# Stores of the transposed blocks and of the softmax heads' outputs: issued from ScalarE's queue in place of SyncE's

## The chip, the cores and the metric

One core of a Trainium2 chip runs the whole program. The metric is the device time of one execution in microseconds. The engines are called by the names of the profile: PE (TensorE), DVE (VectorE), ACT (ScalarE), POOL (GpSimd) and SP (SyncE). Each works through its own list of instructions in order; they wait for one another by semaphores. A DMA is an instruction too: it stands in the list of the engine that issues it, and it is issued when that engine comes to it and its semaphores are there. "SPq" and "ACTq" in the trace are these issues.

## The reference

One layer of a decoder on 512 tokens with 2048 columns, all float32. Cut to what matters:

```python
h = rms_norm(x, norm1_g)
proj = h @ w_in                      # columns of two groups of heads
out_a = gla_mixer(qa, ka, va, ra, log_g, onorm_g)      # 4 heads of gated linear attention
out_b = dilated_mixer(rms_norm(qb), rms_norm(kb), vb, rel_bias)  # 8 softmax heads, 3 dilations
x = x + concat(out_a, out_b) @ w_out
h2 = rms_norm(x, norm2_g)
x = x + (silu(h2 @ w_gate) * (h2 @ w_up)) @ w_down     # 5632 hidden columns
```

## The kernel before

**The products.** All large matrix products go through one scheme. A pair of 512-column blocks of a weight matrix is multiplied for all 512 tokens by seven products of half-sized blocks (`PRODUCTS`, P1 to P7; a Strassen-like scheme), whose left operands are blocks of the activations and sums of them (`A11`, `A12`, `A22`, `S1` to `S4`). Each product runs over up to four groups of 256 rows; one such step is called an item here. For an item the weights (or a difference of two weight blocks, made by DVE at L256) are split in a high part `wh`, which ACT casts (L331), and a rest `wl`, which DVE subtracts (L335). PE multiplies with 8 matmuls that read `wh` and then 4 that read `wl` (L367). `wh` and `wl` have two buffers each, so the cast for the next item can begin when PE has read the `wh` of the item before. The left operands are split in the same way in `Operand.split`: ACT casts (L174), DVE subtracts (L175).

**The stages.** First the projections with `w_in` (to 563 us of the profile), with the attention heads run between the items; then the product with `w_out` (to 734 us), then eleven pairs of `w_gate` and `w_up` (to about 1556 us, called the feed-forward stage here), then `w_down`.

**The turned rows.** A result has tokens on the partitions; the next product needs columns there. `transposed_store` (L1122 to L1145) does this for a 256-token half: for each of two column blocks, 8 transposes on PE (L1129, 4 into each half of a bank), copies from PSUM to a tile on ACT (L1137, or two with a scale at L1140), and a 256 KB store to a DRAM tensor (L1144). It writes three kinds: `mix_d` from the tile `turned` (the gated heads, called from `final_gate`), `xn_d` from `oT` and `PT` (the normalized rows after `w_out`, by `scaled_store`) and `p_d` from `oT` and `PT` (the feed-forward products). Each block is read back in the layout of an operand by `part` (L1193, tiles `r` and `top`) or `fetch_part` (L1237, tiles `v`, `T`, `qT`, `kT`, `oT`, `PT`); such a load waits until the store that it reads has landed.

**The softmax heads.** `dil_head` runs two heads side by side (lanes). ACT copies each 128-column block of the output into `ot` (L1022; the tile is called `oT` in lane 0 and `r` in lane 1), and after the last one `ot` is stored to `mix_d` (L1035). `early_jobs` loads these rows as `top` (L1193) and makes operands of them; `late_jobs` makes the sums.

**The order.** `load` and `store` are both `nc.sync.dma_start`: all loads and stores of the program but three small loads at the start stand in SP's queue, in one order. The program's order on each engine is made by a scheduler from the order of the program text and its own estimates; only the first pair of projections has an order written out by hand. So a change of the issuing engine can also move other instructions.

Of the kernel before, what the change touches and what calls it, by code (L numbers as in the profile page):

```python
# [107 lines left out]
def block_kernel(ctx: ExitStack, tc: tile.TileContext, ins, out):  # L108
    nc = tc.nc
# [18 lines left out]
    def nm(s):  # L128
        uid[0] += 1
        return f"{s}_{uid[0]}"  # L130

    def dram(shape, name):
        return dr.tile(shape, F32, name=name, tag=name)

    def bank():
        return ps.tile([P, 512], F32, name=nm("bank"), tag="bank")

    def work(tag, shape=(P, 512), bufs=1):
        return mp.tile(list(shape), F32, name=nm(tag), tag=tag, bufs=bufs)

    def const(shape, name):
        return cp.tile(list(shape), F32, name=name, tag=name)
# [2 lines left out]

    load = nc.sync.dma_start
    store = nc.sync.dma_start

    mats = const([P, 4, P], "mats")
    ident, tri, stri, causal = (mats[:, i, :] for i in range(4))  # L150
# [229 lines left out]
    def soon(fn, groups=1):  # L380

        soonest.append([groups, fn])
# [445 lines left out]
    mix_d = [dram([P, 2, 512], f"mix_d{b}") for b in range(8)]  # L828

    def head_cols(src, h, w=P):  # L830
        return src.rearrange("(t p) c -> p t c", p=P)[:, :, h * w : (h + 1) * w]
# [117 lines left out]
    def dil_head(h, lane):  # L949


        s = h // 4

        def tile_(name):
            if lane == 0:
                return work("oT" if name == "o" else name)
            if name in "qk":
                return work(name + "T")
            return rpool.tile([P, 512], F32, name=nm("r"), tag="r")

        def logits(b):
            if lane == 0:
                return work("L", bufs=2)
            return tile_("L") if b % 2 else work("PT")

        qh, kh, vh = tile_("q"), tile_("k"), tile_("v").rearrange("p (t d) -> p t d", t=4)
        load(qh.rearrange("p (t d) -> p t d", t=4), head_cols(proj[f"qb{s}"], h % 4))
        load(kh.rearrange("p (t d) -> p t d", t=4), head_cols(proj[f"kb{s}"], h % 4))
        load(vh, head_cols(proj[f"vb{s}"], h % 4))
        tb = tile_("T")  # L970
        load(tb, bass.AP(
            tensor=rep_d.tensor, offset=h * P * NB + P - 1, ap=[[NB - 1, P], [1, 512]]
        ))
        yield
        for src, g in ((qh, gq), (kh, gk)):
            tp = bank()
            for t in range(4):
                nc.tensor.transpose(tp[:, t * P : (t + 1) * P], src[:, t * P : (t + 1) * P], ident)
            nc.scalar.activation(src, tp, AF.Copy, scale=g)
        yield  # L980
        ot = tile_("o")
        lgs = {}

        def scores(b):
            n = P * (b + 1)
            lp = bank()
            nc.tensor.matmul(lp[:, :n], qh[:, b * P : (b + 1) * P], kh[:, :n], start=True, stop=True)  # L987
            lg = lgs[b] = logits(b)
            st = work("mx", (P, 4), bufs=4)

            def rest():
                nc.vector.tensor_tensor_reduce(
                    lg[:, :n], lp[:, :n], tb[:, 512 - n :], -1.0, 3.0e38, ALU.add, ALU.min,
                    st[:, 0:1],
                )
                nc.scalar.activation(
                    lg[:, :n], lg[:, :n], AF.Exp, scale=-1.0, bias=st[:, 0:1],
                    accum_out=st[:, 2:3],
                )

                def scaled():
                    nc.vector.reciprocal(st[:, 3:4], st[:, 2:3])
                    nc.vector.tensor_scalar(lg[:, :n], lg[:, :n], st[:, 3:4], None, op0=ALU.mult)

                soon(scaled)

            return rest

        def turn(b, tp):
            n = P * (b + 1)  # L1010
            for k in range(b + 1):
                nc.tensor.transpose(
                    tp[:, k * P : (k + 1) * P], lgs[b][:, k * P : (k + 1) * P], ident
                )
            return lambda: nc.scalar.copy(lgs[b][:, :n], tp[:, :n])

        def values(b, op):
            for k in range(b + 1):
                nc.tensor.matmul(  # L1019
                    op, vh[:, k, :], lgs[b][:, k * P : (k + 1) * P], start=(k == 0), stop=(k == b)  # L1020
                )
            return lambda: nc.scalar.copy(ot[:, b * P : (b + 1) * P], op)  # L1022

        for i in range(6):
            rests = []
            tp = bank() if 1 <= i <= 4 else None
            if i >= 2:
                op = tp[:, i * P : (i + 1) * P] if i < 4 else bank()[:, :P]
                rests.append(values(i - 2, op))
            if tp is not None:  # L1030
                rests.append(turn(i - 1, tp))
            if i < 4:
                rests.append(scores(i))
            if i == 5:
                rests.append(lambda: store(mix_d[4 + h // 2][:, h % 2, :], ot))  # L1035
            yield rests

    def dil_heads(h):

        lanes = [dil_head(h, 0), dil_head(h + 1, 1)]  # L1040
        for i in range(8):
            for n, lane in enumerate(lanes):
                for rest in next(lane) or ():
                    rest()
                if i == 7 and n == 1:
                    done.update((id(mix_d[4 + h // 2]), half) for half in range(2))
                yield 0.5
            if i == 0 and h % 4 == 0:
                yield
# [72 lines left out]
    def transposed_store(tiles, half, dsts, gains=None, spare=None):  # L1122

        for b in range(2):
            bk = bank().rearrange("p (j n) -> p j n", j=2)
            for jj in range(2):
                for m in range(2):
                    f = (2 * b + jj) * P
                    nc.tensor.transpose(  # L1129
                        bk[:, jj, m * P : (m + 1) * P], tiles[m][:, f : f + P], ident  # L1130
                    )
            if spare is None:
                d = work(("oT", "PT")[b], (P, 2, 256))
            else:
                d = spare[:, b]
            if gains is None:
                nc.scalar.copy(d, bk)  # L1137
            else:
                for jj in range(2):
                    nc.scalar.activation(  # L1140
                        d[:, jj, :], bk[:, jj, :], AF.Copy,
                        scale=gains[:, 2 * b + jj : 2 * b + jj + 1],
                    )
            store(dsts[b][:, :, half * 256 : (half + 1) * 256], d)  # L1144
            done.add((id(dsts[b]), half))  # L1145

    onorm = {}
# [7 lines left out]
    def final_gate(half, which, tiles, acc_):  # L1155
        og = onorm.pop((half, which))
        if tiles is None:
            tiles = [cpool.tile([P, 512], F32, name=nm("cr"), tag="C") for _ in range(2)]
            src = acc_
        else:  # L1160
            src = tiles
        for m in range(2):
            if src is acc_:
                nc.vector.scalar_tensor_tensor(
                    halves(og[m]), unfolded(src[m]), row_scale(half, m), halves(og[m]),
                    op0=ALU.mult, op1=ALU.mult,
                )
                neg = nrs1[:, 2 * half + m : 2 * half + m + 1]
                nc.scalar.activation(halves(tiles[m]), unfolded(src[m]), AF.Exp, scale=neg)
            else:  # L1170
                nc.vector.tensor_tensor(og[m], src[m], og[m], op=ALU.mult)
                nc.scalar.activation(tiles[m], src[m], AF.Exp, scale=-1.0)
            nc.scalar.activation(tiles[m], tiles[m], AF.Ln, bias=1.0)
            nc.scalar.activation(tiles[m], tiles[m], AF.Exp, scale=-1.0)

        def rest():
            for m in range(2):
                nc.vector.tensor_tensor(tiles[m], tiles[m], og[m], op=ALU.mult)
            spare = apool.tile([P, 2, 2, 256], F32, name=nm("turned"), tag="A")
            later(1 + (src is tiles), lambda: transposed_store(  # L1180
                tiles, half, mix_d[2 * which : 2 * which + 2], spare=spare
            ))

        soon(rest, 2)
# [424 lines left out]
```

## Time and profile before

| | |
|---|---|
| median of 3 runs | 1971.18 us (1969.9 to 1972.38) |
| the profiled execution | 1970.09 us, its span 1968.3 us |
| busy: PE, DVE, ACT, POOL | 1927.2, 1653.5, 1094.6, 58.1 us |
| granted TensorE clock | 0.997 |
| DMA traffic | 360.45 MB, mean 183 GB/s |
| packets of SP's queue / of ACT's queue | 236776 / 208 |
| stores of L1144 | 44 of p_d, 16 of xn_d, 8 of mix_d, 256 KB each |
| stores of L1035 | 8 of mix_d, 256 KB each |

The span runs from the first to the last instruction; 1.79 us of the execution lie outside it. A row of the timeline has the start, the duration, the engine, the line of the kernel, the operation, output<-input, a count, and in brackets how long the engine had stood idle before and what ended that. A row of the windows has the length of a stretch and then the busy time of PE, of the weight loads, DVE, ACT and POOL, the granted clock, the DMA engines' busy share and GB/s.

### The profile page before, as it was taken

To read this page: it belongs to the slowest core of one execution; us is meant where nothing else is said; L and a number is where in the kernel's file an instruction comes from. 1 tells how busy PE (TensorE), PEld (TensorE's weight loads), DVE (VectorE), ACT (ScalarE), POOL (GpSimd) and SP (SyncE) were. 2 spreads that over 40 slices of the span, in tenths; PEclk is the share of its full clock that TensorE was granted. 3 is DMA by queue.
4 is the path that set the end of the run, shared out by engine and by line. 5 is a ranking of instruction groups with operands and counts; after the bars stand their busy time and mean duration, and the time that the engine had idled before them with its cause. 6 is when DMAs were issued, how large, how long until landed. Compare 5 with 4: busy or idle time off the path is not lost.

```text
span 1968.3 us, 25787 instructions
## 1 busy us (share of the span) xinstructions
PE 1927.2 (98%) x9226; PEld 1668.3 (85%) x9226; DVE 1653.5 (84%) x1850; ACT 1094.6 (56%) x1600; POOL 58.1 (3%) x81
## 2 busy tenths in 40 slices
PE   7999999999989999999999999999999999999998
PEld 6888888888878887888888888888888888888887
DVE  7997787868779889878878878878879989989987
ACT  7664564566766776545445445545446646546443
POOL 0000230011000000000000000000000000000000
PEclk9999999999999999999999999999999999999999
DMA  8358355464666685554554553554555865955662
GB/s 278 124 167 277 104 181 160 132 207 133 214 214 189 222 290 157 178 167 132 177 171 129 176 164 127 177 164 129 173 162 165 300 209 179 312 183 174 237 214 75
DMA packets 237113, 360.45 MB, mean 183 GB/s; under 512 B 18246, under 2 KB 96783, under 8 KB 236984
## 3 DMA queue, kind: packets, MB, share of 16 engines
q1 hardware_dynamic: 236776, 358.72, 57.2%
q8 instruction: 72, 1.18, 0.3%
q14 instruction: 57, 0.47, 0.1%
q10 hardware_dynamic: 208, 0.08, 0.0%
HBM read 296.59 MB, written 64.51 MB: 183 GB/s over the span
## 4 chain that ended last, share of the span: by engine, by line
PE 76%; DVE 7%; DMA 6%; issue 3%; ACT 1%; SPq 1%; POOL 0%; DVEq 0%; ACTq 0%
PE acc L367 71%; DVE wl L335 2%; DVE wa L256 1%; PE bank L1129 1%; DMA mix_d<-r 1%; DVE AS L175 1%; PE bank L987 1%; DMA q<-in_x 1%; DMA xn_d<-oT 1%; PE bank L1019 1%; DMA q<-y_d 0%; DVE seed L1334 0%; ACT wh L331 0%; DVE seed L294 0%; DMA r<-xn_d 0%
## 5 line engine op out<-in xcount | busy, mean ns | idle before, releaser
L367 PE MATMUL acc<-wh,AS 128*128 128x512 f32 x3008 | 711.3, 379 | 0.6 <-ACT wh L331 0.6
L367 PEld LDWEIGHTS acc<-wh,AS 128*128 128x128 f32 x3008 | 568.2, 189 | 82.5 <-ACT wh L331 1.8
L331 ACT CAST wh<-wa 128x1024 fp32r<-128x1024 f32 x376 | 394.0, 1048 | 390.0 <-PE acc L367 359.9
L367 PE MATMUL acc<-wh,AA 128*128 128x512 f32 x2256 | 534.4, 380 | 0.0
L335 DVE TENSOR_TENSOR wl<-wa,wh 128x1024 fp32r<-128x1024 f32 x376 | 456.8, 1218 | 68.7 <-ACT wh L331 43.6
L367 PEld LDWEIGHTS acc<-wh,AA 128*128 128x128 f32 x2256 | 426.6, 189 | 61.7 <-ACT wh L331 0.8
L367 PE MATMUL acc<-wl,AS 128*128 128x512 f32 x1504 | 395.8, 386 | 9.1 <-DVE wl L335 8.7
L367 PEld LDWEIGHTS acc<-wl,AS 128*128 128x128 f32 x1504 | 278.9, 189 | 62.9 <-DVE wl L335 22.3
L367 PE MATMUL acc<-wl,AA 128*128 128x512 f32 x1128 | 297.4, 386 | 7.4 <-DVE wl L335 7.2
L367 PEld LDWEIGHTS acc<-wl,AA 128*128 128x128 f32 x1128 | 209.2, 189 | 41.1 <-DVE wl L335 11.9
L331 ACT CAST wh<-wb 128x1024 fp32r<-128x1024 f32 x94 | 98.5, 1049 | 129.5 <-PE acc L367 127.8
L331 ACT CAST wh<-wc 128x1024 fp32r<-128x1024 f32 x94 | 98.4, 1047 | 111.8 <-PE acc L367 101.3
L331 ACT CAST wh<-wd 128x1024 fp32r<-128x1024 f32 x94 | 98.5, 1048 | 105.8 <-PE acc L367 102.3
L256 DVE TENSOR_TENSOR wa<-wc,wa 128x1024 f32<-128x1024 f32 x94 | 114.5, 1222 | 47.0 <-DMA wc<-in_w_gate 24.5
L335 DVE TENSOR_TENSOR wl<-wc,wh 128x1024 fp32r<-128x1024 f32 x94 | 114.6, 1219 | 36.0 <-ACT wh L331 35.9
L335 DVE TENSOR_TENSOR wl<-wd,wh 128x1024 fp32r<-128x1024 f32 x94 | 114.4, 1220 | 34.5 <-ACT wh L331 27.6
L335 DVE TENSOR_TENSOR wl<-wb,wh 128x1024 fp32r<-128x1024 f32 x94 | 113.7, 1217 | 5.0 <-ACT wh L331 5.0
L256 DVE TENSOR_TENSOR wb<-wd,wb 128x1024 f32<-128x1024 f32 x94 | 114.5, 1218 | 0.9 <-DMA wd<-in_w_in 0.5
L256 DVE TENSOR_TENSOR wa<-wb,wa 128x1024 f32<-128x1024 f32 x94 | 113.6, 1219 | 0.8
L256 DVE TENSOR_TENSOR wa<-wd,wa 128x1024 f32<-128x1024 f32 x94 | 112.9, 1217 | 0.1
L298 DVE SCALAR_TENSOR_TENSOR seed<-acc,rs,seed 128x512 f32<-128x512 f32 x96 | 70.5, 746 | 24.5 <-PE acc L367 24.5
L282 ACT ACTIVATE seed<-acc,rs 128x512 f32<-128x512 f32 x96 | 60.6, 681 | 1.4 <-PE acc L367 0.8
(303 smaller groups left out, 1364.3 us busy)
## 6 DMA issues: line engine op xcount, KB each, us to landing
wa<-in_w_gate SPq DMA_DIRECT2D x44, 512.0 KB, 4.3
wb<-in_w_up SPq DMA_DIRECT2D x44, 512.0 KB, 4.4
wd<-in_w_up SPq DMA_DIRECT2D x44, 512.0 KB, 4.4
wc<-in_w_gate SPq DMA_DIRECT2D x44, 512.0 KB, 3.6
wc<-in_w_in SPq DMA_DIRECT2D x28, 512.0 KB, 4.1
wa<-in_w_in SPq DMA_DIRECT2D x24, 512.0 KB, 5.4
wb<-in_w_in SPq DMA_DIRECT2D x24, 512.0 KB, 5.7
wd<-in_w_in SPq DMA_DIRECT2D x24, 512.0 KB, 6.0
```

What stands on the lines that cost most here:

```text
L175: nc.vector.tensor_tensor(a[:, :, 1, :], src, a[:, :, 0, :].bitcast(F32), op=ALU.subtract)
L256: nc.vector.tensor_tensor(src, self.quarter(one, g), src, op=ALU.subtract)
L282: nc.scalar.activation(halves(t), unfolded(src[m]), AF.Copy, scale=self.scale(half, m))
L298: nc.vector.scalar_tensor_tensor(halves(seed[m]), unfolded(src[m]), self.scale(half, m), halves(seed[m]), op0=ALU.mult, op1=ALU.add,)
L331: nc.scalar.copy(high[k], sources[k])
L335: nc.vector.tensor_tensor(low[k], sources.pop(k), high[k].bitcast(F32), op=ALU.subtract)
L367: nc.tensor.matmul(p.dst[prod][m], a[:, jj, hl, m * P : (m + 1) * P], folded(w[:, jj, :]), start=fresh and g == 0 and len(terms) == 2 and ...
L987: nc.tensor.matmul(lp[:, :n], qh[:, b * P : (b + 1) * P], kh[:, :n], start=True, stop=True)
L1019: nc.tensor.matmul(op, vh[:, k, :], lgs[b][:, k * P : (k + 1) * P], start=(k == 0), stop=(k == b))
L1129: nc.tensor.transpose(bk[:, jj, m * P : (m + 1) * P], tiles[m][:, f : f + P], ident)
```

## The change

The 68 stores of `transposed_store` and the 8 of `dil_head` are issued by ACT, which also makes the copies that write the stored tiles. Nothing is computed otherwise; all other loads and stores stay on SP.

```diff
     load = nc.sync.dma_start
     store = nc.sync.dma_start
+    store_own = nc.scalar.dma_start
@@ dil_head
             if i == 5:
-                rests.append(lambda: store(mix_d[4 + h // 2][:, h % 2, :], ot))
+                rests.append(lambda: store_own(mix_d[4 + h // 2][:, h % 2, :], ot))
@@ transposed_store
-            store(dsts[b][:, :, half * 256 : (half + 1) * 256], d)
+            store_own(dsts[b][:, :, half * 256 : (half + 1) * 256], d)
             done.add((id(dsts[b]), half))
```

The instruction lists of the two kernels differ as follows. SP's list loses the 76 stores and some of its loads change places, all between 400 and 760 us of the profile before. ACT's list gains them: with copies of one piece (L1137) the two copies come first and the two stores after them; with copies of two pieces (L1140) the store of `oT` stands between the two pieces of `PT`. PE's list has the same instructions in another order in five places between 500 and 740 us, DVE's and ACT's in the stretch from 460 to 790 us; in the feed-forward stage DVE's four sums of `sums_job` (L1483 to L1490) stand one weight split later, some of DVE's weight differences change places in its last pair, and nothing else is moved.

## The prediction

> **What bounds the kernel now.** I read the page's busy times first, then the windows by stage, because an average over stages hides where there is anything to win.
>
> ```profile
> span 1968.3 us, 25787 instructions
> ```
>
> ```profile
> 480.00:520.00 40.00, 38.79 (x207) 33.29 (x207) 29.19 (x54) 26.00 (x54) 0.00 (x0) 1.00 0.46 141
> 520.00:560.00 40.00, 38.48 (x213) 33.02 (x213) 29.10 (x59) 30.95 (x66) 0.00 (x0) 1.00 0.79 255
> 560.00:600.00 40.00, 33.01 (x144) 25.97 (x144) 35.82 (x43) 23.68 (x35) 0.00 (x0) 0.96 0.50 163
> 600.00:640.00 40.00, 39.38 (x182) 34.18 (x182) 39.97 (x47) 24.97 (x37) 0.00 (x0) 1.00 0.68 216
> 640.00:680.00 40.00, 38.01 (x187) 32.06 (x187) 32.81 (x33) 27.43 (x47) 2.97 (x2) 1.00 0.69 239
> 680.00:720.00 40.00, 39.23 (x188) 33.53 (x188) 38.01 (x47) 29.12 (x49) 0.00 (x0) 1.00 0.77 248
> 720.00:760.00 40.00, 33.90 (x158) 27.66 (x157) 33.87 (x43) 27.95 (x48) 4.41 (x5) 1.00 0.78 257
> 830.00:1530.00 700.00, 699.90 (x3310) 611.41 (x3309) 572.35 (x558) 357.55 (x411) 0.00 (x0) 1.00 0.52 160
> ```
>
> The first number after the length is PE. In the feed-forward stretch PE is busy 699.90 of 700 us: nothing that happens to a store there can make the kernel faster, only slower. Between 480 and 760 us PE is idle 1.21 + 1.52 + 6.99 + 0.62 + 1.99 + 0.77 + 6.10 = 19.2 us. That is the largest gain to be had where stores are moved; the first 400 us and `w_down` hold none of them.
>
> The second view is what SP waits for, and the third what a store costs its issuer.
>
> ```profile
> SPq L1144 <- ACT PT L1137: 103.1, 20, 10.4
> ```
>
> ```profile
> L1144 SPq DMA_DIRECT2D p_d<-oT x22: 512/560/1843, 811.8 to 1567.6; - x22
> ```
>
> ```profile
> 1.71 0.50 ACTq L585 DMA_DIRECT2D q<-in_norm_g  x1
> ```
>
> SP stands 103.1 us at the stores of the feed-forward stage, but what follows them in its list are the loads of the same rows, which wait for the stores to land. SP freed of the wait meets that next one at once; I cost it at nothing. The price is the issue: 0.56 us in the middle on SP, and one of ACT's own few DMAs, 16 rows of 512 bytes, took 0.50. For 76 stores ACT gets 76 x 0.56 = 42.6 us, the upper bound if nothing covered it. The lower bound is 0, since an issue runs on the engine's queue and a copy already started can go on beside it.
>
> **Feed-forward stage: 44 stores on ACT, 0 us.**
>
> ```profile
> 811.22 0.58 ACT L1137 COPY oT<-bank 128x512 f32<-128x512 f32 x1
> 811.69 0.59 ACT L1137 COPY PT<-bank 128x512 f32<-128x512 f32 x1
> 813.73 1.05 ACT L331 CAST wh<-wa 128x1024 fp32r<-128x1024 f32 x1 [1.45 <-PE acc L367]
> ```
>
> After the two copies (end 812.28) ACT waits 1.45 us for PE to free a `wh` buffer. The first store can issue while the second copy runs, the second needs 0.56 after it: done at about 812.9, before 813.73. Even both in a row, 1.12 us, fit into 1.45. The cover is that wait; if each store took over 0.73 us the cast would be late, though PE uses it only an item later. DVE's sums of these rows stand one weight split later and read the same loads. So 0, with a bound of +5.5 if the cover broke in all 22 places by a quarter microsecond.
>
> **How long a store takes to land.** The chain of waits goes through stores in the crowded stretch:
>
> ```profile
> 469.34 4.61 DMA mix_d<-r
> 515.04 5.15 DMA mix_d<-r
> 670.83 2.41 DMA xn_d<-oT
> 722.11 5.17 DMA xn_d<-oT
> 736.98 4.45 DMA xn_d<-oT
> ```
>
> With little before it in SP's queue a 256 KB store lands in 2.41 us; behind weight loads of 512 KB in 4.45 to 5.17. From ACT's queue, which carries nothing else, it need not stand behind those loads but still shares the engines with them. No row shows that, so the bounds are 2.4 and 5.2; I take 3.5, a little nearer to the quiet row, because only the waiting goes and not the sharing. The Trainium skill, "DMA: Bandwidth & Descriptors", section "Issuing engines are not separate DMA queues", speaks against a gain here: DMAs from all engines run on the same 16 DMA engines and interleave, and issuing from several saves only the issue time. By it the landing stays at about 5 us, which is the first rival below. The same page, section "Queues, rings and completion order", has each DMA engine take turns between the queues that have work, packet by packet; by that the store would not stand behind the loads. The trace before cannot decide it, with 3 DMAs on ACT.
>
> **469 to 485 us: -0.7.**
>
> ```profile
> 468.06 0.26 ACT L1022 COPY r<-bank 128x128 f32<-128x128 f32 x1
> 473.18 1.05 ACT L331 CAST wh<-wa 128x1024 fp32r<-128x1024 f32 x1 [0.51 <-PE acc L367]
> 477.24 0.63 ACT L174 CAST AA<-top 128x512 fp32r<-128x512 f32 x1 [3.01 <-DMA top<-mix_d]
> 478.18 1.89 PE L367 MATMUL acc<-wh,AS 128*128 128x512 f32 x8
> 481.17 0.49 PE L987 MATMUL bank<-kT,qT 128*128 128x128 f32 x2 [0.67 <-ACT kT L979]
> ```
>
> The copy ends at 468.32, so the store goes at 468.4 instead of 469.34 and lands at 471.9 instead of 473.95; `top` is there 2 us sooner, near 475.2. In the new order this cast of `top` stands ahead of the weight cast that ran at 473.18; that one then ends at about 477, still ahead of 478.18, where PE starts the matmuls that read it. The next weight cast and the copies behind it come 0.7 us sooner, and PE's 0.67 goes. Bounds -1.2 (all idle of the window) and +1 (`top` no sooner, so the cast ends at 478.8 and its `wl` later).
>
> **513 to 535 us: -1.4.**
>
> ```profile
> 513.75 0.27 ACT L1022 COPY r<-bank 128x128 f32<-128x128 f32 x1 [0.52 <-PE bank L1019]
> 524.58 0.69 DVE L215 TENSOR_TENSOR top<-top 128x512 f32<-128x512 f32 x1 [2.10 <-DMA top<-mix_d]
> ```
>
> SP reached the store only at 515.04; ACT can issue it at 514.1. With 3.5 us it lands at 517.6 instead of 520.19 (515.04 + 5.15), DVE's 2.10 us of waiting goes, and DVE is no longer behind in the next 10 us, in which PE stood for it. Nearly all of the window's 1.52. Bounds -1.52 and 0.
>
> **556 to 603 us: +0.5.**
>
> ```profile
> 563.33 0.69 DVE L1251 TENSOR_TENSOR r<-T,r 128x512 f32<-128x512 f32 x1 [4.54 <-DMA r<-mix_d]
> 573.32 1.13 PE L367 MATMUL acc<-wl,AA 128*128 128x512 f32 x4 [1.59 <-DVE wl L335]
> 576.26 2.14 PE L1129 MATMUL bank<-mats,cr 128*128 128x128 f32 x8 [1.81 <-DVE cr L1178]
> ```
>
> DVE loses 4.54 us to a load, not to a store, and has no rest until 603; PE's 7 us of the window follow from that. The load's issue stays where it is. The new order puts the transposes of `cr` ahead of one item on PE, and the casts for `cr` ahead of that item's weight cast on ACT; PE then stands through 571 to 576 with that item still to do (2.6 us later at 580), but DVE, which sets the end of the stretch, comes out only about 0.5 us later, since it has done a weight difference more by then. The 8 stores of `turned` and the last 2 of the heads stand on ACT here behind pairs of copies, with DVE and not ACT as the late engine; they are inside this term. Bounds: -2 (the load shares the engines better) and +3 (the 2.6 us of the item are not absorbed).
>
> **660 to 694 us: +0.65 and -0.8.**
>
> ```profile
> 667.57 1.06 ACT L331 CAST wh<-wa 128x1024 fp32r<-128x1024 f32 x1
> 668.68 1.99 PE L367 MATMUL acc<-wh,AS 128*128 128x512 f32 x8 [0.37 <-ACT wh L331]
> 694.03 1.13 PE L367 MATMUL acc<-wl,AS 128*128 128x512 f32 x4 [0.77 <-DVE wl L335]
> ```
>
> Here ACT is late already: PE waits 0.37 for the cast of 667.57. Two stores now stand ahead of it. Each is issued between copies of other tiles; a copy of 0.4 us runs beside about half of each issue, so 0.33 each, +0.65. Later casts had 2 us to spare. Bounds 0 and 8 x 0.56 = +4.5. The wait of 0.77 at 694 came from a weight load that stood behind row loads on SP; the new order has it ahead of them: -0.8, or 0 at worst.
>
> **720 to 760 us: -2.5.**
>
> ```profile
> 730.89 0.69 DVE L215 TENSOR_TENSOR top<-top 128x512 f32<-128x512 f32 x1 [4.47 <-DMA top<-xn_d]
> 732.77 1.13 PE L367 MATMUL acc<-wl,AA 128*128 128x512 f32 x4 [1.64 <-DVE wl L335]
> 736.13 0.83 ACT L1140 ACTIVATE oT<-bank,g 128x256 f32<-128x256 f32 x2
> 739.53 1.13 PE L367 MATMUL acc<-wl,AA 128*128 128x512 f32 x4 [1.25 <-DVE wl L335]
> 748.00 1.13 PE L367 MATMUL acc<-wl,AA 128*128 128x512 f32 x4 [1.71 <-DVE wl L335]
> ```
>
> The store of 722.11 lands at 725.6 instead of 727.28, the `top` loads come about 1.7 us sooner, and in the new order the weight split that had stood behind DVE's 4.47 us of waiting goes ahead of it, so the 1.64 at 732.77 goes. Against that all four `top` casts now stand ahead of one weight cast on ACT: it waits for the second `top` tile and PE stands about 1.4 there. The copies of 736.13 come 1.5 us sooner, their store lands 3.5 after instead of 4.45, so the sums that PE waited for at 748.00 come some 2.5 sooner. DVE has no rest from there to 768 and keeps the lead: -2.5. Bounds -6.1 (all idle) and +1.6 (landing unchanged and the weight cast late).
>
> **The sum.** -0.7 - 1.4 + 0.5 + 0.65 - 0.8 - 2.5 = -4.25 us. Against the profiled execution, 1970.09 us with its span of 1968.3 and 1.79 around it, that is 1965.8; carried to the median of the runs, 1971.18, it is 1966.9. A measurement of this kernel can tell about 0.2%, 3.9 us, from no change.
>
> **The rivals.** *Landing unchanged.* If a store from ACT's queue lands as late as before, only the earlier issue and the new order remain: -0.7 halves, -1.4 becomes -0.7, the last term becomes +0.4: -0.35 - 0.7 + 0.5 + 0.65 - 0.8 + 0.4 = -0.3, so 1970.9. For it: the windows show the DMA engines at 0.7 to 0.8 in these stretches, so sharing alone may eat the gain. Against: 2.41 beside 5.17 with the same bytes.
>
> *ACT becomes the late engine.* In place: the 16 stores of `xn_d` between 663 and 750 us, where ACT has casts waited for. If an issue is not covered by a copy and delays the next cast whole, that is 16 x 0.56 = 9.0 us, and the stores themselves go later, so that the gain of the last term is gone: -0.7 - 1.4 + 0.5 - 0.8 + 9.0 = +6.6, so 1977.8. Without it the other terms are -0.7 - 1.4 + 0.5 - 0.8 - 2.5 = -4.9, so it turns the sign from 4.9 / 16 = 0.31 us of late cast for each store there; I have counted 0.33 for two stores and nothing for the other 14. For it: the 0.37 above, and ACT busy 27.4 to 29.1 of 40 us in these windows. Against: the casts after 672 had room.
>
> *The new order.* The moved casts behind `cr` and behind `top` cost their bounds, +3 and +1.6, with the other terms -0.7, -1.4, +0.65, -0.8: +2.3, so 1973.5; it counts with the small changes.
>
> **How the numbers follow.** Forecast, faster by over 0.2%: 0.41, its own range 1961 to 1967.2. Landing unchanged or the new order, within 0.2%: 0.24 together with the cases between. ACT late: 0.35, since it gathers every place where I called an issue half covered, and no row shows an ACT store. The range reaches from 1961 (beyond -4.25, with more of the 6.1 and the 6.99) to 1978, the price of ACT late.
>
> **What would show it.** Right: stores as ACTq rows of about 0.56 us, `mix_d<-r` and `xn_d<-oT` landing in 3 to 4 us, DVE's waits of 2.10 and 4.47 short or gone, the feed-forward window still at 699.9. Wrong: PE waits for `wh` growing between 660 and 690, ACT issues well over 0.56, landings still near 5, or idle in the feed-forward stage.

## The result: 0.2% slower, and the profile after

The changed kernel takes 1975.98 us in the median (1972.89 to 1978.78, 17 runs); the kernel before, run beside it, 1971.19 us (1968.59 to 1975.84, 17 runs). The ratio is 1.0021, 95% interval 1.0014 to 1.0027: slower by 2.8 to 5.3 us, where 4.25 us of gain were forecast. The page of the changed kernel:

```profile
span 1972.4 us, 25780 instructions
```

Its lines after 147 stand one higher than before's (L332 is before's L331). Its windows, to be held against those of the prediction:

```profile
520.00:560.00 40.00, 39.23 (x217) 33.75 (x217) 29.40 (x60) 32.05 (x69) 0.00 (x0) 1.00 0.81 261
560.00:600.00 40.00, 32.52 (x144) 27.01 (x143) 35.64 (x43) 23.72 (x36) 0.00 (x0) 0.87 0.49 162
600.00:640.00 40.00, 38.77 (x179) 33.32 (x178) 39.99 (x47) 25.78 (x37) 0.00 (x0) 1.00 0.71 227
680.00:720.00 40.00, 40.00 (x195) 35.16 (x194) 36.97 (x46) 30.69 (x49) 0.00 (x0) 1.00 0.76 244
720.00:760.00 40.00, 32.72 (x144) 27.25 (x144) 32.43 (x42) 26.65 (x47) 4.94 (x5) 0.91 0.75 254
830.00:1530.00 700.00, 699.83 (x3313) 613.21 (x3312) 572.60 (x558) 357.72 (x412) 0.00 (x0) 1.00 0.52 159
```

From 520 on, 720 to 760 lost most: PE busy 32.72 us against 33.90, and the granted clock 0.91 against 1.00. At a lower clock the same matmuls count as busy for longer, so the loss is larger than these 1.18 us. 560 to 600 and 600 to 640 lost 0.49 and 0.61, 520 to 560 and 680 to 720 gained 0.75 and 0.77. To say how much was lost where, I use two marks that lie in every version: the first PE transpose of an `L` tile (the second half of `w_out` begins its turned rows) and the first of a `seed` tile after it (the first feed-forward rows). The rows of the transposes, first and last start in us, before:

```profile
L1129 PE MATMUL bank<-mats,L x48: 272/273/331, 659.3 to 743.4; 128*128 128x128 f32 x48
L1129 PE MATMUL bank<-mats,seed x16: 272/272/273, 810.1 to 822.1; 128*128 128x128 f32 x16
```

and after:

```profile
L1130 PE MATMUL bank<-mats,L x48: 272/273/332, 659.7 to 745.1; 128*128 128x128 f32 x48
L1130 PE MATMUL bank<-mats,seed x16: 272/273/273, 814.1 to 826.1; 128*128 128x128 f32 x16
```

Between the marks lie 810.1 - 659.3 = 150.8 us before and 814.1 - 659.7 = 154.4 after: 3.6 us are lost there, 0.4 ahead of it, and the spans differ by 4.1. I call this length *the stretch* below. It doesn't carry the spread of the rest of the run, but it comes from one trace for each version. Five versions below leave all orders between the marks as they were (heads only, turned rows only, feed-forward only, all but `xn_d`, turned rows with feed-forward); with the kernel before they give 150.7 to 152.2 us. So 3 us tell versions apart here, and 1.5 us do not.

What happens in it is seen in ACT's list. After:

```profile
731.23 0.62 ACT L175 CAST AA<-top 128x512 fp32r<-128x512 f32 x1 [1.39 <-DMA top<-xn_d]
732.03 0.62 ACT L175 CAST AS<-top 128x512 fp32r<-128x512 f32 x1 [0.18 <-DVE top L216]
732.83 0.62 ACT L175 CAST AA<-top 128x512 fp32r<-128x512 f32 x1 [0.19 <-DMA top<-xn_d]
734.83 0.62 ACT L175 CAST AS<-top 128x512 fp32r<-128x512 f32 x1 [1.38 <-DVE top L216]
735.36 1.04 ACT L332 CAST wh<-wa 128x1024 fp32r<-128x1024 f32 x1
```

and before:

```profile
731.61 0.62 ACT L174 CAST AS<-top 128x512 fp32r<-128x512 f32 x1 [0.18 <-DVE top L215]
732.14 1.04 ACT L331 CAST wh<-wa 128x1024 fp32r<-128x1024 f32 x1
734.65 0.62 ACT L174 CAST AA<-top 128x512 fp32r<-128x512 f32 x1 [1.48 <-DMA top<-xn_d]
```

The weight cast, the first of the feed-forward stage, ran at 732.14 behind two of the four casts of `top`; now it stands behind all four and runs at 735.36. PE after:

```profile
736.45 3.78 PE L368 MATMUL acc<-wh,AA 128*128 128x512 f32 x8 [4.71 <-ACT wh L332]
740.02 1.91 PE L368 MATMUL acc<-wl,AA 128*128 128x512 f32 x4
749.34 1.13 PE L368 MATMUL acc<-wl,AA 128*128 128x512 f32 x4 [2.21 <-DVE wl L336]
```

PE stands 4.71 us for that cast, and the 12 matmuls behind the wait then run at about half speed: 3.78 and 1.91 us, where the rows of the prediction have 1.89 and, behind a short wait, 1.13. The granted clock from 736 to 740 us is 0.50. At 749 it waits again, behind sums that DVE makes of loads. These come late because of the landings, in the chain of waits (start, us):

```profile
469.72 4.33 DMA mix_d<-r
722.88 6.79 DMA xn_d<-PT
737.17 6.84 DMA xn_d<-oT
744.03 3.26 DMA r<-xn_d
```

The store of 737 lands in 6.84 us where the one at the same place took 4.45, and the loads of `r` begin at 744.03 instead of 741.45. None of these landings came near the 3.5 us that the prediction took. The quiet ones were below it: the stores of `oT` issued from 665 to 711 us landed in 2.7 us in the middle.

SP's list shows a further difference. Before, one weight load (733.04) stood closely ahead of the store of 736.98, and the next two behind it (738.88 and 743.86). SP no longer waits for that store, and in the new order these two are issued at 734.51 and 735.21, ahead of the store of 737.17.

Two causes offered themselves, and a third from the prediction's rivals. **ORDER**: the scheduler's new order on ACT. **LANDING**: a store from ACT's queue lands later when loads are in flight; that SP is free to issue loads earlier belongs to it. **ISSUE**: ACT's half microsecond for each store delays its casts. The row of these issues (shortest, middle and longest in ns):

```profile
L1145 ACTq DMA_DIRECT2D xn_d<-oT x8: 520/521/521, 665.7 to 749.5; - x8
```

### The profile page after: what moved, and what is told of

The parts are those of the page before. It is cut to its first block, busy times and chain, and to the rows that moved or that the text cites. A ratio compares the mean times of both kernels' runs of the same rounds, so it can differ in the third digit from the quotient of the medians.

```text
span 1972.4 us, 25780 instructions
## 1 busy us (share of the span) xinstructions
PE 1930.2 (98%) x9226; PEld 1674.2 (85%) x9226; DVE 1653.3 (84%) x1850; ACT 1097.5 (56%) x1600; POOL 58.8 (3%) x81
## 3 DMA queue, kind: packets, MB, share of 16 engines
q8 instruction: 72, 1.18, 0.3%
## 4 chain that ended last, share of the span: by engine, by line
PE 80%; DVE 6%; DMA 3%; issue 2%; ACT 2%; POOL 0%; SPq 0%; ACTq 0%; DVEq 0%
PE acc L368 75%; DVE wl L336 3%; PE bank L1130 1%; DVE wa L257 1%; PE bank L1020 1%; PE bank L988 1%; ACT wh L332 1%; DVE AS L176 1%; DMA mix_d<-r 1%; PE bank L1013 0%; DMA top<-mix_d 0%; DMA xn_d<-oT 0%; DMA xn_d<-PT 0%; DMA wc<-in_w_down 0%; PE bank L923 0%
## 5 line engine op out<-in xcount | busy, mean ns | idle before, releaser
L332 ACT CAST wh<-wa 128x1024 fp32r<-128x1024 f32 x376 | 393.8, 1048 | 396.1 <-PE acc L368 349.5
L332 ACT CAST wh<-wb 128x1024 fp32r<-128x1024 f32 x94 | 98.6, 1049 | 130.3 <-PE acc L368 126.8
L332 ACT CAST wh<-wc 128x1024 fp32r<-128x1024 f32 x94 | 98.4, 1047 | 113.6 <-PE acc L368 105.7
L332 ACT CAST wh<-wd 128x1024 fp32r<-128x1024 f32 x94 | 98.6, 1048 | 108.6 <-PE acc L368 105.2
```

Source lines behind the costliest of these rows:

```text
L332: nc.scalar.copy(high[k], sources[k])
```

## The experiments

Each ratio below is to the kernel before, run beside on the same chip, with its 95% interval; the microseconds are the ratio's part of 1970.

**1. Which stores.** `gains` is given only for `xn_d`, `spare` only for `turned`.

```diff
-            store_own(dsts[b][:, :, half * 256 : (half + 1) * 256], d)
+            (store_own if gains is not None else store)(dsts[b][...], d)   # xn_only; heads on SP
+            (store_own if gains is None else store)(dsts[b][...], d)       # not_xn
```

> Only the 16 stores of xn_d go on ACT's queue; the stores of mix_d and of p_d stay on SP. Theory ORDER (the loss arises at 730 to 737 us, because all four casts of top stand ahead of one weight cast on ACT): this kernel has that order, so +3.5 to +5 us against the kernel before (about 1975.5), with a wait of PE for wh of more than 4 us near 732. Theory LANDING (a store from ACT's queue lands 1.5 to 2 us later in the crowded stretch) and theory ISSUE (0.52 us of ACT for each store delays the casts): the same +3 to +5, since the late places are all at xn_d. Theory EVERYWHERE (the loss adds up from small pieces at mix_d, xn_d and p_d): under +2.

> All stores of the change on ACT's queue but the 16 of xn_d, which stay on SP. ORDER, LANDING and ISSUE as far as they place the loss at xn_d: -1 to +1.5 us against the kernel before (the profile of the changed kernel stands 1.0 late at 669 us, 0.1 late at 707). EVERYWHERE: +2 or more.

Measured: `xn_d` alone 1.0019 (1.0010 to 1.0027), +3.7 us, stretch 155.5. All but `xn_d` 0.9993 (0.9984 to 1.0002), -1.4 us, stretch 150.7. The 16 stores of `xn_d` cost all that the change costs; "everywhere" is out.

The other kinds by themselves (same edit, one condition each):

> Only the 16 stores of the softmax heads' outputs on ACT's queue, all turned rows on SP. The prediction's terms at 469 and at 513 us: -2.1 us; the run with all but xn_d on ACT gave -1.4. If the quiet stretch lets them land sooner: -0.5 to -3, with the DVE wait of 2.10 us at 524 gone. If nothing is won there either: -0.5 to +1.

(The heads' stores are 8, not 16 as the expectation says.)

> Only the 8 stores of the gate's turned rows into mix_d on ACT's queue. The prediction's term at 556 to 603 us: +0.5. With landings that share with the loads: 0 to +2; the PE window of 560 to 600 us shows it (33.0 to 34.4 us busy in the runs with these stores on SP, 32.5 to 33.0 in the runs with them on ACT).

> Only the 44 stores of the feed-forward stage on ACT's queue. All theories: 0, within -1.5 to +1.5 us, PE busy 699.8 or more of the 700 us from 830; a loss of 2 us or more would mean that their issue on ACT costs something after all.

Measured: heads 0.9995 (0.9986 to 1.0004), stretch 151.2; turned rows 0.9991 (0.9982 to 1.0000), stretch 152.2; feed-forward stores 0.9990 (0.9981 to 0.9999), -2.0 us. The last one warns: PE is busy 700.00 of the 700 us there, against 699.90 before, so that stage has no place where 2 us could have been won, and the profiled span is 1969.1, longer than before's 1968.3. The expectation of at most 1.5 us either way was missed; differences of 2 us at the edge of their interval are not explained here, and I build on nothing that rests on them alone.

**2. ORDER without the queue.** All stores on SP; the edit holds only the weight cast, behind the last cast of `top`. The scheduler moves more with it: on SP two weight loads (733.58 and 734.12) now stand ahead of the store of 736.98, which goes at 739.43, and some of DVE's differences and of ACT's copies change places. So this is a new order and not one cast.

```diff
+            if p.op is opn and prod == "P1" and g == 0 and ("S1", 2) not in p.op.t:
+                with tc.issue_after(recent["cast"]):
+                    nc.scalar.copy(high[k], sources[k])
```

> All stores on SP's queue as before; only one cast on ACT is moved: the first weight cast of the feed-forward stage stands behind the last of the four casts of top. ORDER: PE waits 3.5 to 5 us for that wh near 732 and the kernel is 3 to 5 us slower than before. LANDING and ISSUE: 0 to +1.6 us, as the prediction's bound for that move alone, since no store lands or is issued differently.

Measured: 1.0013 (1.0005 to 1.0022), +2.6 us, stretch 154.4, as long as in the changed kernel. PE's row, and the landing in the chain:

```profile
738.72 3.78 PE L372 MATMUL acc<-wh,AA 128*128 128x512 f32 x8 [3.46 <-ACT wh L334]
```

```profile
722.53 5.31 DMA xn_d<-oT
```

The wait of 3.46 us and the 3.78 of slow matmuls are there with the store landing in 5.31 us from SP. ORDER is a cause without any store on ACT; its +2.6 lies below the 3 to 5 that it expected, and above the +1.6 that LANDING and ISSUE had at most, with an interval (1.0 to 4.3 us) that reaches into both.

**3. The order undone, stores on ACT.** In `early_jobs` the casts of `opn`'s tops are taken up some items later:

```diff
+            for _ in range(2):
+                if op is opn:
+                    soon(lambda job=job: next(job), 6)
+                else:
+                    next(job)
+                yield 0.5
```

> All stores on ACT's queue as in the changed kernel; the casts of the two top tiles of the feed-forward stage's groups 2 and 3 are taken up some items later, so that only one of them stands ahead of the first weight cast. ORDER: PE's wait for wh near 732 falls from 4.7 to about 1.2 us and its slow matmuls behind it go; 3 to 5 us faster than the changed kernel, about 1971. LANDING: the sums of r stay late at 748 us (2.2 us of waiting for wl), so at most 2 us come back, 1974. ISSUE: nothing comes back, 1975.5.

Measured: 1.0022 (1.0013 to 1.0031), +4.3 us, stretch 154.3. The 4.71 us of waiting for `wh` fell to 0.56, and nothing came back. That would speak against ORDER as the only cause, if the edit itself were free. The chain has

```profile
720.87 5.79 DMA xn_d<-oT
733.03 6.32 DMA xn_d<-oT
```

and PE now waits in small pieces, 1.48 and 1.38 for `wl` and 1.26 for `L`, with one slow run of 8 matmuls (3.56 us). The same edit with all stores on SP:

> All stores on SP; the casts of the two top tiles are taken up as late as in the run that moved them with the stores on ACT (+4.3 us there). LANDING: the loss of that run came from the late landing, so here -2 to +1 us against the kernel before. If the late casts themselves cost it (PE waits for wl, L and slow matmuls at 735 to 750): +3 to +4.5 us again.

Measured: 1.0013 (1.0003 to 1.0024), +2.6 us, stretch 152.7. Moving the casts so far has a price of its own (PE waits 0.96 and 1.29 for the operands `AA` that now come late), so this pair separates the two causes badly: 154.3 against 152.7 leaves 1.6 us for the stores' queue, hardly more than the stretch varies by itself. A cleaner pair was needed.

**4. LANDING with the old order.** With only the last 8 stores of `xn_d` on ACT (those from 715 us on), the scheduler leaves the casts near 730 in the order of before. On SP, which no longer waits for these stores, weight loads come earlier: one at 721.15, ahead of the store of 722.03 instead of behind it, and two at 734.50 and 735.52, ahead of the one of 737.82.

```diff
+            own = gains is None or dsts[0] is xn_d[4] or dsts[0] is xn_d[6]
+            (store_own if own else store)(dsts[b][:, :, half * 256 : (half + 1) * 256], d)
```

> All stores of the change on ACT's queue but the first 8 of xn_d, which stay on SP. ACT's casts near 730 us then stand in the order of the kernel before (one weight cast between the casts of the two top tiles), while the last 8 stores of xn_d, those of 722, 737 and behind, go from ACT's queue. ORDER alone: no loss, -1.5 to +1 us against the kernel before, as the run with all xn_d on SP. LANDING (on ACT's queue these stores land in 5.8 to 6.8 us, on SP's in 4.2 to 5.3): the top loads and the sums at 745 to 748 us come 1.5 to 2 us late, +2 to +4 us.

Measured: 1.0016 (1.0007 to 1.0025), +3.2 us, stretch 153.7. The chain, then PE:

```profile
722.03 6.81 DMA xn_d<-oT
737.82 5.70 DMA xn_d<-oT
```

```profile
751.55 2.08 PE L367 MATMUL acc<-wl,AA 128*128 128x512 f32 x4 [4.16 <-DVE wl L335]
```

No wait for `wh` at 732; instead the sums are late and PE stands 4.16 us at 751. So these stores, with the loads that now go ahead of them, cost about as much as the new order, in another place. The counterpart, the first 8 on ACT:

> All stores of the change on ACT's queue but the last 8 of xn_d, which stay on SP. ACT's order near 730 us has three casts of top ahead of the weight cast instead of two before and four in the changed kernel. ORDER: PE waits 1 to 3 us for wh near 732, +1 to +2.5 us. LANDING: the stores at 722 and 737 land in 4.2 to 5.3 us as before, -1 to +1 us. ISSUE at the first 8 stores: +0.6 at 668 us and no more.

Measured: 1.0008 (0.9999 to 1.0017), stretch 153.8. Three casts of `top` stand ahead of the weight cast, PE waits 2.98 us for it. The time can't be told from no change; the stretch is 3.0 longer. The wait for `wh` looks like ORDER again, but the expected landings of 4.2 to 5.3 us were missed too:

```profile
723.06 7.31 DMA xn_d<-PT
```

This store and its partner of 722.40 (7.3 us) went from SP's queue, with weight loads issued at 719.98 and 721.93, later than before's 718.31 and 719.62. So a landing as late as from ACT's queue also occurs on SP, here with the loads closer ahead of the store; what each part costs here was not separated.

**5. ISSUE.** First a try that misled: an extra DMA of 256 pieces of 4 bytes from ACT behind each of the last 8 pairs of copies, stores on SP.

```diff
+            if gains is not None and (dsts[0] is xn_d[4] or dsts[0] is xn_d[6]):
+                nc.scalar.dma_start(dram([P, 2, 1], nm("spare_d")), d[:, :, 0:1])
```

> All stores on SP. Behind each of the last 8 pairs of copies for xn_d, ACT issues a further DMA of 256 pieces of 4 bytes to a spare buffer, so that ACT pays the issue where it paid it with the stores, but no store changes its queue, and the casts near 730 us keep the order of the kernel before. ISSUE: the casts behind come late, +2 to +4 us as with the last 8 stores on ACT (+3.2). LANDING: -1 to +1 us.

Measured: 1.0181 (1.0165 to 1.0197), +36 us, which neither theory had. The small pieces are no free stand-in: from 715 to 790 us they land in 11.8 and 14.5 us, and the 256 KB stores beside them need as long, 11.2 and 14.4. It says nothing on ISSUE. In its place, a small copy with a sum on ACT where the issues would stand:

```diff
+                nc.scalar.activation(idle[:, 8:88], d[:, 1, 176:256], AF.Copy, accum_out=idle[:, q_ : q_ + 1])
```

> All stores on SP. At the places where ACT issued the last 8 stores of xn_d it now runs a small copy with a sum (about 0.4 to 0.5 us of ACT) that nothing waits for; the casts near 730 us keep the order of the kernel before. ISSUE: +2 to +4 us, as with these stores on ACT (+3.2). LANDING: -1 to +1 us, since no store lands otherwise.

Measured: 1.0009 (1.0000 to 1.0018), +1.8 us, stretch 150.5. The copies and the marks:

```profile
739.41 0.26 ACT L1150 ACTIVATE idle<-oT 128x80 f32<-128x80 f32 x1
739.58 0.19 ACT L1150 ACTIVATION_READ_ACCUMULATOR idle<-oT 128x1 f32 x1
```

```profile
L1131 PE MATMUL bank<-mats,L x48: 272/273/331, 661.7 to 745.7; 128*128 128x128 f32 x48
L1131 PE MATMUL bank<-mats,seed x16: 272/272/273, 812.2 to 824.2; 128*128 128x128 f32 x16
```

The time lies between the two expectations, but 812.2 - 661.7 = 150.5 us is no longer than before's 150.8: where the copies stand, nothing was lost. The profiled run is late by 2.4 us already at the first mark, ahead of any changed instruction. So ISSUE isn't seen in the trace, and by the time it is at most 3.5 us; ACT has room there. The same 8 stores from GpSimd's queue:

```diff
+            (store_own if gains is None else nc.gpsimd.dma_start if own else store)(dsts[b][...], d)
```

> As the run with the last 8 stores of xn_d on ACT (+3.2 us), but these 8 are issued by GpSimd, on a queue of its own; ACT pays nothing for them, and the stores of mix_d and p_d stay on ACT. LANDING, as the sharing with the loads: still +2 us or more, the stores of 722 and 737 landing in 5.7 us or longer. ISSUE: -2 to +0.5.

Measured: 1.0038 (1.0026 to 1.0051), +7.5 us, stretch 157.4; the stores land in

```profile
xn_d<-oT POOLq DMA_DIRECT2D x4, 256.0 KB, 5.5
```

5.5 us in the middle. It speaks against ISSUE on ACT, but it isn't clean: two of these stores now stand in GpSimd's list behind its own small operations and go only at 753 us.

**6. A store by itself.** Nothing of the block is computed. One store, with two weight loads of 512 KB ahead of it, behind it, or both; from SP in one queue with them, or from ACT.

> Nothing of the block is computed: the output is left with zeros. One 256 KB store of two 1 KB rows a partition, issued by SP (sp...) or by ACT (act...), landing measured to the load that reads it back; alone, behind two weight loads of 512 KB (behind), ahead of two (ahead), or between two and two (both); six times each. If a store on its own queue shares the DMA engines with every load in flight, and one on SP's queue stands only behind what was issued before it: alone 2.4 us on both; behind 4.5 to 6 on SP and 3.5 to 5 on ACT; ahead 2.4 to 3 on SP and 3.5 to 5 on ACT; both 4.5 to 6 on SP and 5 to 8 on ACT. If the own queue only takes away the standing behind, as the prediction took it: ACT 2.4 to 3.5 everywhere.

The rows of the DMA view, the last number the median us from issue to landing, and then the issues of one store that stands ahead of its loads in the program, from each queue:

```profile
spalone<-t SPq DMA_DIRECT2D x6, 256.0 KB, 2.5
actalone<-t ACTq DMA_DIRECT2D x6, 256.0 KB, 2.4
spbehind<-t SPq DMA_DIRECT2D x6, 256.0 KB, 5.0
actbehind<-t ACTq DMA_DIRECT2D x6, 256.0 KB, 5.6
spahead<-t SPq DMA_DIRECT2D x6, 256.0 KB, 2.8
actahead<-t ACTq DMA_DIRECT2D x6, 256.0 KB, 5.6
spboth<-t SPq DMA_DIRECT2D x6, 256.0 KB, 5.1
actboth<-t ACTq DMA_DIRECT2D x6, 256.0 KB, 6.2
```

```profile
33.82 0.56 SPq L59 DMA_DIRECT2D spahead<-t  x1
34.48 1.11 SPq L50 DMA_DIRECT2D w<-in_w_gate  x2
41.07 0.88 SPq L50 DMA_DIRECT2D w<-in_w_gate  x2
41.52 0.52 ACTq L59 DMA_DIRECT2D actahead<-t  x1
```

This is the disputed price. From SP the store pays for the loads issued ahead of it (2.5 to 5.0) and next to nothing for those issued behind it (2.8). From ACT's queue the rows "behind" and "ahead" are one and the same case, a store beside two loads: nothing holds SP's loads back until the store is issued, so they start some 0.45 us before it in both, and both land in 5.6. The own queue didn't take the standing behind away (5.6 beside the loads, 5.0 behind them), and it gave up the place ahead (2.8). Four loads around the store instead of two add 0.6 (6.2). What a store from ACT pays that is really issued before the loads was not measured. The sharing was expected and is there in every row from ACT with loads; its 5.6 lies above the 3.5 to 5 expected for two loads.

**7. Why sharing costs so much.** The store's pieces are 1 KB, the loads' 2 KB. The same with a store laid out in pieces of 2 KB:

> Nothing of the block is computed: the output is left with zeros. The store of 256 KB ahead of two weight loads of 512 KB, or between two and two, as in the run that measured the store by itself, now in pieces of 1 KB (one) or of 2 KB as the loads have (two). If the queues take turns piece by piece: 5.6 and 6.2 us from ACT with 1 KB, 3.5 to 4.8 with 2 KB; SP's 2.8 and 5.1 change by less than 0.5. If they share by bytes or the store stands behind the loads anyway: no difference between the pieces.

```profile
actaheadone<-t ACTq DMA_DIRECT2D x6, 256.0 KB, 5.7
actaheadtwo<-t ACTq DMA_DIRECT2D x6, 256.0 KB, 4.4
actbothone<-t ACTq DMA_DIRECT2D x6, 256.0 KB, 6.2
actbothtwo<-t ACTq DMA_DIRECT2D x6, 256.0 KB, 4.5
```

With pieces as large as the loads' the landing from ACT falls by 1.3 and 1.7 us, and from SP it doesn't change (2.6 and 2.5 ahead, 5.1 and 5.1 between). That fits queues which take turns by pieces, so that the one with the smaller pieces gets the smaller share of the bytes; the expectation had said so, and sharing by bytes would have made no difference. Even so the place ahead of the loads, 2.5 us, was had only on SP. In the kernel: `xn_d` laid out by halves, so that its stores and loads go in 2 KB, with the last 8 on ACT as in experiment 4.

```diff
-            load(t, src[:, :, half * 256 : (half + 1) * 256])
+            load(as_half(src, t), half_of(src, half))      # src[:, half, :] for xn_d, else as before
```

> As the run with the last 8 stores of xn_d on ACT in the old order of casts (+3.2 us, landings of 6.81 and 5.70 us), but xn_d is laid out by halves of the rows, so that its stores and the loads of it go in pieces of 2 KB instead of 1 KB. If the turns piece by piece make these stores late: landings of 4.4 to 5.5 us at 722 and 737 and 1.5 us or more of the 3.2 come back (-1 to +1.7 against the kernel before). If the late landing is not what costs the 3.2: +2 to +4 as without the larger pieces.

Measured: 0.9995 (0.9986 to 1.0004), -1.0 us, stretch 151.2. The landings fell by about 1 and 0.8 us:

```profile
721.50 5.83 DMA xn_d<-oT
736.86 4.89 DMA xn_d<-oT
```

and the 3.2 us are gone. The stores' issues also fell, from 0.52 to 0.33 us. All of it would be credited to the landing by this run alone; the last two runs say that it isn't so.

**8. A faster version.** The stores that gave no loss on ACT (turned rows and the feed-forward stage), the heads and `xn_d` on SP, with 1 KB and with 2 KB pieces for `xn_d`.

> On ACT's queue the 8 stores of the gate's turned rows and the 44 of the feed-forward stage, which gave -1.8 and -2.0 us by themselves (each barely outside no change); on SP the heads' and those of xn_d. If both are real and add: -2.5 to -4. If they are the spread of the runs, as the profile of the second suggests (PE busy 700 of 700 us there before and after): -1.5 to +1.

> As the run with the gate's turned rows and the feed-forward stores on ACT (-1.9 us), with xn_d on SP and laid out for pieces of 2 KB. A store by itself landed from SP in 2.5 instead of 2.6 us and 5.1 as before, so nothing or little more: -4 to -1 against the kernel before.

Measured: with 1 KB 0.9990 (0.9981 to 0.9999), 1967.47 us, stretch 151.0; with 2 KB 0.9975 (0.9964 to 0.9986), 1966.43 us beside 1970.70, 4.9 us faster than the kernel before and by the two ratios some 9 faster than the changed kernel. Its marks:

```profile
L1136 PE MATMUL bank<-mats,L x48: 272/273/332, 657.4 to 739.9; 128*128 128x128 f32 x48
L1136 PE MATMUL bank<-mats,seed x16: 272/272/273, 806.5 to 818.5; 128*128 128x128 f32 x16
```

The stretch is 149.1 us. So the larger pieces win also with the stores on SP (4.9 against 2.0 us, with intervals of 2.8 to 7.1 and 0.2 to 3.7), more than was expected, and with the same pieces SP's queue is still ahead of ACT's: 149.1 against 151.2 in the stretch, 1966.43 against 1969.42 us in runs side by side. (These two differ in the heads' stores as well, which had shown no effect by themselves.) With 1 KB the last 8 stores on ACT stood 5.2 us behind the version with them on SP (+3.2 against -2.0, each against the kernel before run beside it), with 2 KB 3.0. So the larger pieces took away perhaps 2 us of what ACT's queue costs, with wide intervals, and the layout by itself did the rest. The layout pays by itself; it didn't make ACT's queue the better place. How much of its gain comes from the landings and how much from the loads of `xn_d`, which go in larger pieces too, stays open.

## Why the prediction was wrong, point by point

**The failing step is the landing.** "I take 3.5, a little nearer to the quiet row, because only the waiting goes and not the sharing." The waiting didn't go: a store on its own queue beside two loads took 5.6 us where 5.0 behind them was the price on SP. And the loads that had stood behind the store in SP's list were no longer held back by it; they went ahead of it, where on SP they had cost next to nothing (2.8). In the crowded stretch it was 6.8, outside the bounds of 2.4 and 5.2. The upper bound was the row of before, as if the change could only help. How the 6.8 divides into sharing and into the loads that now go ahead stays open.

**720 to 760, -2.5:** it came out near +3.6. The gain of the earlier loads fell with the landing. The loss of the new order had been seen ("all four `top` casts now stand ahead of one weight cast") and priced at 1.4 us of standing, +1.6 in the bound with the landing unchanged; with all stores on SP it cost 3.46 us of waiting and half-speed matmuls behind it, +2.6 in time. The price left out that the last of these casts waits for DVE's difference (1.38 us), which waits for the last load of `top` (2.11), and that PE is slow after such a wait. The two losses don't add up: ORDER alone gave a stretch of 154.4, the late stores alone 153.7, both 154.4. They hide one another, as far as the stretches show it; that the same operands are late either way is the likely reason and not shown by itself. Experiment 3, which undid one of them and got nothing back, doesn't settle it, since its edit costs 2.6 us of its own.

**The other terms.** 469: the landing fell from 4.61 to 4.33, no term of -0.7. 513: DVE's wait of 2.10 fell to 1.16 and PE's busy time rose from 38.48 to 39.23, half of the 1.4; with the heads' stores alone on ACT (-1.0 us, -2.8 to +0.8) the 2.1 us of the first two terms can be neither seen nor ruled out. 556 to 603: +0.5 was right within what can be read (the last waits end at 603.25 and 604.79, with PE 0.8 late at 529 already). 660 to 694: +0.65 and -0.8 were right, PE's wait of 0.37 for `wh` became 0.94 and the 0.77 at 694 is gone (40.00 of 40 us). The feed-forward stage: 0 was right, 699.83.

**The rivals.** *Landing unchanged* had the right mechanism against the forecast and too mild a price. By the Trainium skill, "DMA: Bandwidth & Descriptors", section "Issuing engines are not separate DMA queues", a second queue saves only the issue time; the store by itself agrees where it is alone (2.4 and 2.5), and it is worse than that rule where loads follow in the program (5.6 against 2.8). Its section "Queues, rings and completion order" has the DMA engines take turns between queues packet by packet. The prediction read it as no longer standing behind the loads; the runs with two sizes of pieces fit the turns, and show their other side. *The new order* was counted among the small changes and is one of the two causes. *ACT becomes the late engine* gave the 0.35 for slower and its 1977.8 lies near the 1975.98 measured, but that is luck, its mechanism isn't the one: the issues are 0.52 us, as counted, and the same time put on ACT left the stretch as it was.

## What to carry to other kernels

A store that the chain waits for belongs in the queue whose later loads it holds back: from one queue it landed in 2.8 us ahead of them, from another in 5.6 beside them. Where nothing else is in flight the queue hardly matters (2.5 and 2.4). Where a change of the issuing engine also moves other instructions, price the new order by the wait at its end and by what is slow behind it, and run it without the other change: here it cost 2.6 us with no store on another engine. Two losses at one place can hide one another, so undo them singly and together, and look at a stretch between two marks of the trace, not only at the total; versions that leave that stretch alone show how far it varies by itself.

## What the runs showed of the hardware that I had not expected

PE can come back slow from a wait. After 3.46, 4.71 and 7.83 us of standing (experiment 2, the changed kernel, the small pieces of experiment 5), 8 matmuls took 3.78 us each time instead of 1.89; after waits of 1.64 and 2.21 us the first 4 ran at their 1.13. The length of the wait doesn't settle it alone: behind 1.87 us (experiment 2) 4 matmuls took 1.84, and behind 3.08 us (`xn_last_2k`) 4 ran in 1.13 and the next 8 in 1.89. The Trainium skill, "TensorE: Matmul & The Clock Gate", section "Part 1: The HAM clock gate (the "warmup" mystery)", has the array fall to half its clock after an idle window of about 3.4 us that runs freely; the long waits agree, with a granted clock of 0.50 from 736 to 740 us in the changed kernel. Why the wait of 1.87 us was followed by slow matmuls no run here shows. In the changed kernel the slow matmuls cost PE nearly 3 us on top of the wait: 3.78 - 1.89 in the first row and 1.91 - 1.03 in the next (1.03 is what 4 take without a wait).

A DMA of 256 pieces of 4 bytes, 1 KB in all, took 11.8 to 14.5 us to land, and the 256 KB stores beside such DMAs took 11.2 and 14.4 where the chain before has 4.45 and 5.17.
